# Two RWKV layers: small products of TensorE regrouped, R projections and the bonus term moved earlier, the two halves of the tail set further apart

## The chip, the cores and the metric

One NeuronCore of one Trainium2 chip runs the whole program. The metric is the device time of one execution in microseconds (us). 256 tokens of width 1024 go through four blocks (RWKV, stick-breaking attention, sparse attention, RWKV), each followed by a feed-forward network, and then through two hybrid attention layers. Everything is float32.

## What is computed

The change touches only the two RWKV-7 blocks (16 heads of 64 channels). Cut to what matters:

```python
r, k, v = projections of three mixes of h and its shifted copy      # 1024 x 1024 each
decay = exp(-exp(-softplus(-(w0 + tanh(xw @ w1) @ w2)) - 0.5))      # LoRA of rank 64
a = sigmoid(a0 + (xa @ a1) @ a2)                                    # LoRA of rank 64
g = sigmoid(xg @ g1) @ g2                                           # gate, rank 160 = 128 + 32
kk = k * k_k, divided per head by the root of its sum of squares
state = state * decay - (state @ kk) (kk * a)^T + v k^T             # per token, per head
y = state @ r                                                        # then a norm per head
y = y * ln_w + ln_b + sum(r * k * r_k) * v                           # the bonus term
out = (y * g) @ w_out
```

## The kernel before

The recurrence is done in two chunks of 128 tokens: within a chunk a triangular 128x128 system per head is inverted. Large products are written as three `fp32r` matmuls of a high and a low half (lines 117 to 119), and `wload` (L110, L111) splits each weight block of 128x1024 on ScalarE (`whi`) and VectorE (`wlo`). Plain float32 matmuls are two passes on TensorE each, so the counts of matmul rows below are passes, twice the matmuls in the code. Instructions are written in Python order; the framework's planner then orders each engine's queue by that order and by what its model says is ready, so neighbours in the trace need not be neighbours in the code. One RWKV layer (`rwkv`) goes through these stages:

- **Gate and LoRAs.** `lora1` (L1008) makes the gate's inner product in one go: for each of 8 row blocks k, a matmul with 128 columns of weights and one with 32. Its two sigmoids give `sg1` (128 rows) and `sg2` (32 rows). Then a loop over pairs of channel blocks makes decay and `a` (L1066, L1067) with sigmoids on ScalarE and a scan on VectorE (L1074).
- **K projections.** `kproj(c)` for channel block c is 24 matmuls, a copy and a square on ScalarE, and a matmul with `headsel` (L1126: 8 columns) that adds the squares per head into one PSUM tile of 8 rows for four blocks. `rnorm(j)` turns it into inverse norms, `prep` spreads them with a selection matrix (L1139, L1140).
- **The block loop** (L1195 to L1205) over c = 0 to 7: `prep(c+1)` on VectorE and ScalarE, `amat(c)` (L1165, transposes, masked copies), then a K projection for c = 0 and 1 or an R projection for c = 3 and 6 (`RPC`), then `wmat(c)` (L1184).
- **Inversion.** `inv_diag` inverts 32x32 blocks by a chain of 62 VectorE operations (L1330, L1332), each waiting for the one before. Meanwhile the other six R projections (`rproj`, L1253) and the products `rmat` (L1225) and `rout` (L1237, L1243) run.
- **Merge.** `inv_merge` joins the blocks with small matmuls (L1360, L1374, L1376, L1384, L1387). Between its steps it calls `turn()`, which here makes a quarter of the gate's second product (`gtc`, L1266 with 128 rows and L1267 with 32 rows).
- **Tail.** `rwkv_tail(q)` is a Python generator for each half q of the heads. Half B starts two steps (`RLAG`) after half A. In it the bonus term `bv` is built (L1476, L1478). `ohalf` is the output projection; its first half is handed out two pieces per step (`RFO`) once A is done.

```python
for c in range(RPN, KT):                 # L1251: the six later R projections
    rproj(re, c)
    for _ in range(RFR[c]):
        rph.pop(0)()                     # rmat / rout
```

Of the kernel before, what the change touches and what calls it, by code (L numbers as in the profile page):

```python
# [23 lines left out]
RPC = (3, 6)  # L24
RPN = len(RPC)
RFR = (0, 0, 2, 2, 2, 2, 3, 3)
RLAG, RFA, RFB, RFO = 2, 0, 0, 2
# [4 lines left out]
GTP = {}  # L32
# [10 lines left out]
class Prog:  # L43
# [864 lines left out]
    def rwkv(self, x, i):  # L908
# [13 lines left out]
        with ExitStack() as outer:  # L922
# [13 lines left out]
            sg2 = sp.tile([32, S], F32, name="sg2")  # L936
            rnh = [sp.tile([8, S], F32R, name=f"rnh{j}") for j in range(2)]
            rnl = [sp.tile([8, S], F32R, name=f"rnl{j}") for j in range(2)]
# [7 lines left out]
            with tc.tile_pool(name="ra", bufs=1) as ra:  # L946
# [55 lines left out]
                def lora1(m, w, o, n, stride):  # L1002
                    ps = self.psum("mm")
                    for k in range(KT):
                        t = mix(m, k, "xg_", 8)
                        for q in range(0, n, 128):
                            p = min(128, n - q)
                            mm(ps[:p, q // 128 * S:q // 128 * S + S], w[:, o + k * stride + q:o + k * stride + q + p], t,  # L1008
                               start=(k == 0 and q == 0), stop=(k == KT - 1), skip_group_check=True)
                    return ps  # L1010
# [48 lines left out]
                ps = lora1(5, G1, 0, 160, 160)  # L1059
                act(sg1, ps[:, :S], AF.Sigmoid)  # L1060
                act(sg2, ps[:32, S:], AF.Sigmoid)
                for c0 in range(0, KT, 2):
                    pw, pa = self.psum("mm"), self.psum("at")
                    for c in (c0, c0 + 1):
                        o = (c - c0) * S
                        mm(pw[:, o:o + S], L2[:64, c * 128:(c + 1) * 128], la[:64], start=True, stop=True)  # L1066
                        mm(pa[:, o:o + S], L2[64:, c * 128:(c + 1) * 128], la[64:], start=True, stop=True)  # L1067
                    for c in (c0, c0 + 1):
                        o = (c - c0) * S
                        sg = ra.tile([128, S], F32, name="sg", bufs=2)  # L1070
                        act(sg, pw[:, o:o + S], AF.Sigmoid, bias=C("w0", c))
                        act(aT[:, c], pa[:, o:o + S], AF.Sigmoid, bias=C("a0", c))
                        nc.gpsimd.memset(csT[:, c, 0:1], 0.0)
                        nc.vector.tensor_tensor_scan(csT[:, c, 1:], self.ones, sg, 0.0, op0=ALU.mult, op1=ALU.add)  # L1074
                ctr = csT[:, :, 64:256:128]
# [27 lines left out]
            with tc.tile_pool(name="rb", bufs=2) as rb:  # L1103
                self.table("natural_log_exp_and_others")
                selr = rb.tile([8, 4, 128], F32, name="selr", tag="akk1", bufs=1)
                nc.sync.dma_start(selr, self.a["rw_sel8"])
                sel8 = rb.tile([8, 4, 128], F32R, name="sel8", bufs=1)
# [4 lines left out]
                kw, ssp = [None], [None]  # L1112
                nc.gpsimd.tensor_scalar(ka1, C("k_a", 0, 8), -1.0, 1.0, op0=ALU.mult, op1=ALU.add)

                def kproj(c):
                    if c % 2 == 0:
                        kw[0] = self.wload(self.a["rw_k"][l, c // 2], 2048)
                    if c % 4 == 0:
                        ssp[0] = self.psum("o")[:8, :S]
# [4 lines left out]
                    sq = self.tmp.tile([128, S], F32, name="sq", bufs=2)  # L1124
                    act(sq, ps, AF.Square, scale=C("k_k", c))
                    mm(ssp[0], headsel[:, c % 4], sq, start=(c % 4 == 0), stop=(c % 4 == 3))  # L1126

                def rnorm(j):
                    u = self.tmp.tile([128, S], F32, name="sacc", bufs=2)[:8]
                    ts(u, ssp[0], 1e-24, 2.0 ** 20, op0=ALU.max, op1=ALU.mult)  # L1130
                    rn = self.rstd(u, scale=1.0, eps=0.0, p=8)
# [56 lines left out]
                rp = iter(range(RPN))  # L1188
# [6 lines left out]
                for c in range(KT):  # L1195
# [7 lines left out]
                    elif c in RPC:  # L1203
# [3 lines left out]
                act(scol, scol, AF.Exp)  # L1207
            with ExitStack() as rde:
# [4 lines left out]
                re = rde.enter_context(tc.tile_pool(name="re", bufs=2))  # L1213
# [41 lines left out]
                self.xctx.close()  # L1255
                rt = rde.enter_context(tc.tile_pool(name="rt", bufs=1, side="right"))
                GT = rt.tile([128, KT, S], F32, name="GT")
                g2 = self.wraw.tile([128, WCH], F32, name="wraw")
                nc.sync.dma_start(g2[:, :1024], self.a["rw_g2a"][l])
                nc.sync.dma_start(g2[:32, 1024:], self.a["rw_g2b"][l])  # L1260

                def gtc(c0):
                    pg = self.psum("mm")
                    for c in (c0, c0 + 1):
                        o = (c - c0) * S
                        mm(pg[:, o:o + S], g2[:, c * 128:128 + c * 128], sg1, start=True, stop=False)  # L1266
                        mm(pg[:, o:o + S], g2[:32, 1024 + c * 128:1152 + c * 128], sg2, start=False, stop=True)  # L1267
                    cp(GT[:, c0:c0 + 2], pg.rearrange("p (a b) -> p a b", a=2))
                TT.append(rt.tile([128, 16, 128], F32, name="TT1"))
                act(TT[1], self.ones[:, None, :128].to_broadcast([128, 16, 128]), AF.Copy, scale=0.0)  # L1270
# [5 lines left out]
                self.inv_merge([u.rearrange("p a h t -> p (a h) t") for u in AKB], XNT, TT, sc, lambda: gts.pop(0)())  # L1276

                def chain(q):
                    return self.rwkv_tail(q, rc, rt, l, mu, Vc, AKB[q], KB, TT[q], csT, Rh, N0, W00, WK1, scol, coef, GT,
                                          sc[q], C, og, lambda: [rph.pop(0)() for _ in range(max(0, len(rph) - 8 * (1 - q)))],  # L1280
                                          lambda: [gts.pop(0)() for _ in range(max(0, len(gts) - 2 * (1 - q)))])
                add = lambda c, ps: self.new_x(c, x[c], ps)
                fills = [rph, gts, []]

                def fill(n):
                    for _ in range(n):
                        for f in fills:
                            if f:
                                f.pop(0)()
                                break  # L1290
                A, B, i = chain(0), chain(1), 0
                while A or B:
                    if A:
                        if next(A, 1):
                            A = None
                            fills[2] = self.ohalf(self.a["rw_out"][l], 0, og, add)
                        fill(RFA)
                    if B and i >= RLAG:
                        if next(B, 1):
                            B = None  # L1300
                        fill(RFB if A else RFO)
                    for _ in range(GTP.get(i, 0)):
                        if gts:
                            gts.pop(0)()
                    i += 1
                for f in fills[2] + self.ohalf(self.a["rw_out"][l], 1, og, add):
# [99 lines left out]

    def rwkv_tail(self, q, rc, rt, l, mu, Vc, AKB, KB, TT, csT, Rh, N0, W00, WK1, scol, coef, GT, scr, C, og, need, need_gate):

# [21 lines left out]
        need()  # L1430
# [18 lines left out]
        for g in range(2):  # L1449
# [3 lines left out]
            (nc.vector.tensor_copy if g else cp)(UP[:, 4 * g:4 * g + 4], ps)  # L1453
# [19 lines left out]
        bv = TT.rearrange("p h t -> p (h t)")[:, :1024].rearrange("p (c a e v) -> p c a e v", c=4, a=2, e=2)  # L1473
        for ch in range(2):
            bc = lambda u: u[:, ch, hq].rearrange("p (c e) -> p c e", e=2)[:, :, :, None].to_broadcast([128, 4, 2, 64])
            tt(out=bv[:, :, ch], in0=Vc[:, ch, 512 * q:512 * q + 512].rearrange("p (c e v) -> p c e v", e=2, v=64),  # L1476
                                    in1=bc(mu), op=ALU.add)
            tt(out=bv[:, :, ch], in0=bv[:, :, ch], in1=bc(coef), op=ALU.mult)  # L1478
# [12 lines left out]
        need_gate()  # L1491
# [91 lines left out]
def layout(inp, need=None):  # L1583
# [81 lines left out]
    out["rw_g2a"], out["rw_g2b"] = np.ascontiguousarray(f("rw_g2")[:, :128]), np.ascontiguousarray(f("rw_g2")[:, 128:])  # L1665
# [5 lines left out]
    hsel = np.zeros((128, 4, 8), np.float32)  # L1671
    for ch in range(128):
        for cc_ in range(4):
            hsel[ch, cc_, 2 * cc_ + ch // 64] = 1.0
    out["rw_headsel"] = hsel
    out["rw_sel8"] = np.ascontiguousarray(1024.0 * hsel.transpose(2, 1, 0))
# [42 lines left out]
```

## Time and profile before

| | us |
|---|---|
| median of 3 runs | 1864.0 (1863.23 to 1868.2) |
| the profiled execution, its own time | 1852.14 |
| span of its trace, first to last instruction | 1850.4 |
| first RWKV layer, up to the first matmul of the network after it | 273 |
| second RWKV layer, the same stages | 273 |
| mean granted clock of TensorE, share of 2.4 GHz | 0.952 |

The profiled execution is 0.6% below the median of the runs. The engines are TensorE (PE, its weight loads PEld), VectorE (DVE), ScalarE (ACT), GpSimd (POOL) and SyncE (SP), which issues most of the DMAs. A stage of the trace is read by its windows first (which engine is full), then by the timeline or the chain of waits inside it. In the timeline a row is the start in us, the length in us, the engine, the line, what is written and read, the form, the count, and in brackets the idle time before it and what ended that. Successive matmuls overlap, so the price of one in a stream is the distance between starts.

### The profile page before, as it was taken

To read this page: it belongs to the slowest core of one execution; us is meant where nothing else is said; L and a number is where in the kernel's file an instruction comes from. 1 tells how busy PE (TensorE), PEld (TensorE's weight loads), DVE (VectorE), ACT (ScalarE), POOL (GpSimd) and SP (SyncE) were. 2 spreads that over 40 slices of the span, in tenths; PEclk is the share of its full clock that TensorE was granted. 3 is DMA by queue.
4 is the path that set the end of the run, shared out by engine and by line. 5 is a ranking of instruction groups with operands and counts; after the bars stand their busy time and mean duration, and the time that the engine had idled before them with its cause. 6 is when DMAs were issued, how large, how long until landed. Compare 5 with 4: busy or idle time off the path is not lost.

```text
span 1850.4 us, 34035 instructions
## 1 busy us (share of the span) xinstructions
PE 1756.0 (95%) x13699; PEld 1575.6 (85%) x13699; DVE 1375.6 (74%) x2710; ACT 1013.8 (55%) x1832; POOL 40.5 (2%) x78
## 2 busy tenths in 40 slices
PE   7998989999999999999999989999899998997998
PEld 5677789999899999877999966787899997885876
DVE  8869489866688876799887568686787656676665
ACT  4755345545576455567645445754265445664664
POOL 0003000000000000000000000021000000000000
PEclk9989789999999999999999999886899999998999
DMA  5211138746427855632685542211065455432540
GB/s 214 103 52 55 59 113 323 259 157 228 168 93 279 288 183 172 237 137 92 239 295 191 182 164 102 73 57 47 35 223 188 170 192 193 160 137 91 181 159 23
DMA packets 52841, 292.19 MB, mean 158 GB/s; under 512 B 6611, under 2 KB 9435, under 8 KB 27980
## 3 DMA queue, kind: packets, MB, share of 16 engines
q1 hardware_dynamic: 48540, 284.64, 43.4%
q10 hardware_dynamic: 4144, 5.39, 0.9%
q8 instruction: 107, 1.75, 0.4%
q14 instruction: 50, 0.41, 0.1%
HBM read 287.90 MB, written 2.10 MB: 157 GB/s over the span
## 4 chain that ended last, share of the span: by engine, by line
PE 73%; DVE 14%; DMA 5%; ACT 3%; issue 2%; DVEq 0%; ACTq 0%
PE mm L117 14%; PE mm L118 14%; PE mm L119 14%; PE mm L222 5%; PE mm L223 5%; PE mm L224 5%; DMA adaw<-ada 4%; DVE wlo L111 3%; DVE junk L678 2%; PE o L511 1%; PE at L475 1%; PE mm L1184 1%; PE at L1165 1%; PE mm L1266 1%; PE mm L1267 1%
## 5 line engine op out<-in xcount | busy, mean ns | idle before, releaser
L111 DVE TENSOR_TENSOR wlo<-wraw,whi 128x1024 fp32r<-128x1024 f32 (+2 forms) x518 | 588.3, 1140 | 229.5 <-ACT whi L110 227.3
L110 ACT CAST whi<-wraw 128x1024 fp32r<-128x1024 f32 (+2 forms) x518 | 504.2, 982 | 296.9 <-PE mm L119 174.3
L222 PE MATMUL mm<-whi,xgh 128*128 128x512 f32 x192 | 80.9, 421 | 8.5 <-ACT xgh L737 8.5
L1549 ACT ACTIVATE sg<-gt 128x256 f32<-128x256 f32 x88 | 36.7, 417 | 90.0 <-DVE gt L1546 89.8
L117 PE MATMUL mm<-mh,whi 128*128 128x256 f32 x256 | 80.9, 316 | 5.0 <-DVE Rh L1097 3.8
L118 PE MATMUL mm<-mh,wlo 128*128 128x256 f32 x256 | 77.9, 304 | 0.0
L119 PE MATMUL mm<-ml,whi 128*128 128x256 f32 x256 | 77.8, 304 | 0.0
L223 PE MATMUL mm<-wlo,xgh 128*128 128x512 f32 x192 | 77.2, 402 | 0.0
L224 PE MATMUL mm<-whi,xgl 128*128 128x512 f32 x192 | 77.0, 402 | 0.0
L678 DVE SCALAR_TENSOR_TENSOR junk<-adaw,cs 128x1024 f32<-128x1024 f32 x48 | 58.6, 1221 | 17.9 <-DMA adaw<-ada 17.7
L1546 DVE TENSOR_TENSOR gt<-mm,rr 128x512 f32<-128x512 f32 x88 | 60.5, 687 | 8.5 <-PE mm L119 5.7
L117 PEld LDWEIGHTS mm<-mh,whi 128*128 128x128 f32 x256 | 55.2, 216 | 9.0 <-DVE Rh L1097 4.0
L118 PE MATMUL mm<-xg0h,wlo 128*128 128x256 f32 x192 | 53.8, 280 | 5.2 <-DVE wlo L111 5.1
L118 PEld LDWEIGHTS mm<-mh,wlo 128*128 128x128 f32 x256 | 55.2, 216 | 1.7 <-issue 1.7
L119 PEld LDWEIGHTS mm<-ml,whi 128*128 128x128 f32 x256 | 54.7, 214 | 1.7 <-issue 1.7
L117 PE MATMUL mm<-xg0h,whi 128*128 128x256 f32 x192 | 54.6, 284 | 0.0
L119 PE MATMUL mm<-xg7l,whi 128*128 128x256 f32 x192 | 53.2, 277 | 0.6 <-DVE xg7l L135 0.6
L222 PEld LDWEIGHTS mm<-whi,xgh 128*128 128x128 f32 x192 | 37.4, 195 | 18.9 <-ACT xgh L737 9.4
L117 PE MATMUL mm<-xg4h,whi 128*128 128x256 f32 x192 | 53.5, 278 | 0.0
L117 PE MATMUL mm<-xg7h,whi 128*128 128x256 f32 x192 | 53.2, 277 | 0.0
L119 PE MATMUL mm<-xg0l,whi 128*128 128x256 f32 x192 | 53.1, 277 | 0.0
L117 PE MATMUL mm<-xg1h,whi 128*128 128x256 f32 x192 | 53.1, 277 | 0.0
(831 smaller groups left out, 6067.1 us busy)
## 6 DMA issues: line engine op xcount, KB each, us to landing
wraw<-ffn_gu SPq DMA_DIRECT2D x88, 1024.0 KB, 6.1
wraw<-ffn_dn SPq DMA_DIRECT2D x64, 704.0 KB, 4.0
adaw<-ada SPq DMA_DIRECT2D x48, 512.0 KB, 5.7
wraw<-hy_qkv SPq DMA_DIRECT2D x24, 1024.0 KB, 4.9
wraw<-rw_k SPq DMA_DIRECT2D x8, 1024.0 KB, 4.9
wraw<-rw_r SPq DMA_DIRECT2D x8, 1024.0 KB, 4.9
wraw<-rw_out SPq DMA_DIRECT2D x8, 1024.0 KB, 4.8
wraw<-sb_qk SPq DMA_DIRECT2D x8, 1024.0 KB, 4.8
```

Source lines behind the costliest of these rows:

```text
L110: nc.scalar.copy(hi, rw)
L111: nc.vector.tensor_tensor(out=lo, in0=rw, in1=hi.bitcast(F32), op=ALU.subtract)
L117: mm(ps, w[0], x[0], start=first, stop=False, **kw)
L118: mm(ps, w[1], x[0], start=False, stop=False, **kw)
L119: mm(ps, w[0], x[1], start=False, stop=last, **kw)
L222: mm(ps, x[0], w[0], start=first, stop=False)
L223: mm(ps, x[0], w[1], start=False, stop=False)
L224: mm(ps, x[1], w[0], start=False, stop=last)
L475: nc.tensor.matmul(z[e][:, o:o + n], qT[b, hp, t * 128:t * 128 + 128], kT[b, hp, :n], start=True, stop=True)
L678: nc.vector.scalar_tensor_tensor(out=junk, in0=raw, scalar=1.0, in1=self.cs, op0=ALU.mult, op1=ALU.mult, accum_out=self.mod[l][:, j:j + 1])
L1546: nc.vector.tensor_tensor(out=gt, in0=ps.rearrange("p (a b) -> p a b", a=2), in1=r[:, None, :].to_broadcast([128, 2, S]), op=ALU.mult)
L1549: nc.scalar.activation(sg, gt[:, 0], AF.Silu)
```

## The change

The gate's inner product is cut in four pieces that are spread over the LoRA loop, and its 32-column part is made four times, into PSUM rows 0, 32, 64 and 96. The squares of k stay in the second half of `KB`, and four matmuls with a 32-column `headsel` in `rnorm` write to the four row quarters. `gtc` makes four channel blocks at a time, with the 32-row parts on four row groups and four PSUM tiles. All eight R projections are in the block loop. `GT`, `TT1` and the loads of `g2` come before the `rmat`/`rout` products. The bonus term is made by eight VectorE operations ahead of `inv_turn`, in a pool opened after that of `rmat`/`rout` is closed. `RLAG` goes from 2 to 5.

```diff
-RPC = (3, 6)
+RPC = (0, 0, 1, 1, 1, 1, 2, 2)
-RLAG, RFA, RFB, RFO = 2, 0, 0, 2
+RLAG, RFO = 5, 2
...
-                def lora1(m, w, o, n, stride):
+                def lora1(ps, ks, m, w, o, n, stride):
+                    for k in ks:
+                        xt_ = [(k + j, mix(m, k + j, "xg_", 8)) for j in range(2)]
                         for q in range(0, n, 128):
                             p = min(128, n - q)
+                            for k1, t in xt_:
+                                for g in range(0, 128, p):
+                                    mm(ps[g:g + p, q // 128 * S:q // 128 * S + S], w[:, o + k1 * stride + q:o + k1 * stride + q + p], t,
+                                       start=(k1 == 0 and q == 0), stop=(k1 == KT - 1), skip_group_check=True)
...
-                ps = lora1(5, G1, 0, 160, 160)
+                pg = self.psum("mm")
                 for c0 in range(0, KT, 2):
...
+                    lora1(pg, (c0,), 5, G1, 0, 160, 160)
+                act(sg1, pg[:, :S], AF.Sigmoid)
+                act(sg2, pg[:, S:], AF.Sigmoid)
...
-                    act(sq, ps, AF.Square, scale=C("k_k", c))
-                    mm(ssp[0], headsel[:, c % 4], sq, start=(c % 4 == 0), stop=(c % 4 == 3))
+                    act(KB[:, c, S:], ps, AF.Square, scale=C("k_k", c))
                 def rnorm(j):
+                    ssp = self.psum("o")[:, :S]
+                    for c in range(4):
+                        mm(ssp[32 * c:32 * c + 32], headsel, KB[:, 4 * j + c, S:], start=True, stop=True)
...
-                    elif c in RPC:
+                    for _ in range(RPC[c]):
                         rproj(rb, next(rp))
...
+                def gtc(a):
+                    pg = [self.psum("at")[:, :S] for _ in range(4)]
+                    for j in range(4):
+                        c = 4 * a + j
+                        mm(pg[j], g2[:, c * 128:128 + c * 128], sg1, start=True, stop=False)
+                    for j in range(4):
+                        b = slice(32 * j, 32 * j + 32)
+                        mm(pg[j], g2[b, 1024 + a * 128:1152 + a * 128], sg2[b], start=False, stop=True)
+                    for j in range(4):
+                        cp(GT[:, 4 * a + j], pg[j])
...
-                for c in range(RPN, KT):
-                    rproj(re, c)
-                    for _ in range(RFR[c]):
-                        rph.pop(0)()
+                for j, f in enumerate(rph):
+                    f()
+                    if j == 8:
+                        gtc(0)
+                rex.close()
+                bv = rde.enter_context(tc.tile_pool(name="rv", bufs=1)).tile([128, 2, 4, 2, 2, 64], F32, name="bv")
+                for q in range(2):
+                    for ch in range(2):
...
+                        tt(out=bv[:, q, :, ch], in0=Vc[...], in1=bc(mu), op=ALU.add)
+                        tt(out=bv[:, q, :, ch], in0=bv[:, q, :, ch], in1=bc(coef), op=ALU.mult)
...
-                og, gts = [None] * KT, [lambda c=c: gtc(c) for c in range(0, KT, 2)]
+                og, gts = [None] * KT, [lambda: gtc(1)]
```

The host's layout follows: `rw_g2b` is 128 rows of 256 values instead of 32 of 1024, `rw_headsel` is 128x32, and `rw_sel8` has 128 rows instead of 8.

## Rows read from the trace of the kernel before

**Rows 1.** The page, part 1: busy time, share and instructions of each engine.
```profile
PE 1756.0 (95%) x13699; PEld 1575.6 (85%) x13699; DVE 1375.6 (74%) x2710; ACT 1013.8 (55%) x1832; POOL 40.5 (2%) x78
```
**Rows 2.** Windows: length, busy PE PEld DVE ACT POOL, PEclk, DMA; last row second layer.
```profile
61.50:88.50 27.00, 23.32 (x160) 19.18 (x160) 18.16 (x35) 21.87 (x47) 1.11 (x3) 0.94 0.32 121
88.50:138.40 49.90, 46.52 (x338) 40.19 (x339) 35.49 (x89) 26.81 (x79) 1.03 (x2) 0.83 0.13 46
138.40:181.50 43.10, 37.30 (x344) 35.09 (x343) 41.35 (x84) 25.87 (x60) 17.20 (x19) 0.95 0.18 62
181.50:216.70 35.20, 33.15 (x480) 23.65 (x480) 12.31 (x17) 14.57 (x21) 0.00 (x0) 0.57 0.14 43
216.70:273.20 56.50, 50.88 (x482) 49.13 (x481) 45.93 (x103) 22.52 (x47) 0.00 (x0) 0.91 0.25 96
1174.40:1224.90 50.50, 47.48 (x337) 40.86 (x338) 35.52 (x89) 26.82 (x79) 1.03 (x2) 0.80 0.14 45
```
**Rows 3.** Groups by line, VectorE, inversion (138.4 to 181.55): busy us, mean ns.
```profile
L111 DVE TENSOR_TENSOR wlo<-wraw,whi 128x1024 fp32r<-128x1024 f32 x5 | 6.1, 1216 | 0.0
...
L1097 DVE TENSOR_TENSOR Rh<-mm,E1r 128x256 f32<-128x256 f32 x6 | 2.5, 411 | 0.0
```
**Rows 4.** The chain that ended last, merge: start, us, what.
```profile
183.55 3.82 PE mm L1360 x128
187.37 1.15 PE mm L1266 x2
...
212.27 0.63 PE mm L1266 x2
...
214.77 2.00 PE at L1387 x32
```
**Rows 5.** Windows: most of the merge.
```profile
183.00:211.00 28.00, 27.45 (x414) 19.41 (x416) 8.82 (x14) 12.89 (x19) 0.00 (x0) 0.50 0.12 39
```
**Rows 6.** Timeline of TensorE, tail.
```profile
243.74 1.12 PE L1498 MATMUL mm<-ident,WK 128*128 128x128 f32 x4 [3.38 <-DVE WK L1446]
```
**Rows 7.** Timeline of TensorE: an unbroken float32 stream, and the gate's inner product.
```profile
33.01 3.62 PE L1054 MATMUL mm<-dx,L1m 128*128 128x256 f32 x16
...
47.66 9.39 PE L1008 MATMUL mm<-xm,G 128*128 128x256 f32 x32
```
**Rows 8.** Timeline of TensorE, tail: products that alternate between two column halves.
```profile
228.79 1.09 PE L1468 MATMUL at<-KB,AKB 128*64 128x128 f32 x16
```
**Rows 9.** Timeline of TensorE: head sums among K projections, and the first L1165.
```profile
68.28 0.97 PE L1126 MATMUL o<-sq,rw_headsel 128*8 128x256 f32 x2 [1.96 <-ACT sq L1125]
...
72.63 0.60 PE L1126 MATMUL o<-sq,rw_headsel 128*8 128x256 f32 x2
...
83.26 0.60 PE L1126 MATMUL o<-sq,rw_headsel 128*8 128x256 f32 x2
...
88.52 1.80 PE L1165 MATMUL at<-aT,KB 64*128 64x128 f32 x16 [1.42 <-DVE KB L1155]
```
**Rows 10.** Timeline of TensorE, block loop: five of the wmat groups, one rout.
```profile
94.33 1.00 PE L1184 MATMUL mm<-Vc,akk 128*128 128x64 f32 x8
...
100.84 1.00 PE L1184 MATMUL mm<-Vc,akk 128*128 128x64 f32 x8
...
106.39 0.88 PE L1184 MATMUL mm<-Vc,akk 128*128 128x64 f32 x6
...
114.34 1.00 PE L1184 MATMUL mm<-Vc,akk 128*128 128x64 f32 x8
...
117.17 0.51 PE L1237 MATMUL o<-rkb,prod 128*128 128x2 f32 x4
...
119.38 0.88 PE L1184 MATMUL mm<-Vc,akk 128*128 128x64 f32 x6
```
**Rows 11.** Groups by line, VectorE, tail (216.7 to 258): the bonus term.
```profile
L1476 DVE TENSOR_TENSOR TT<-Vc,mu 128x512 f32<-128x512 f32 x4 | 2.7, 688 | 2.0 <-PE mm L1425 2.0
L1478 DVE TENSOR_TENSOR TT<-TT,coef 128x512 f32<-128x512 f32 x4 | 2.7, 684 | 0.0
```

More of the change, by code (lines that the diff above doesn't have):

```diff
@@ L935, in rwkv @@
             sg1 = sp.tile([128, S], F32, name="sg1")
[L936 to L938 removed]
+            sg2 = sp.tile([128, S], F32, name="sg2")
+            rnh = [sp.tile([128, S], F32R, name=f"rnh{j}") for j in range(2)]
+            rnl = [sp.tile([128, S], F32R, name=f"rnl{j}") for j in range(2)]
             mu = sp.tile([128, 2, 16], F32, name="mu")
@@ L1212, in rwkv @@
                 X = self.inv_diag(rd, AKB)
-                re = rde.enter_context(tc.tile_pool(name="re", bufs=2))
+                rt = rde.enter_context(tc.tile_pool(name="rt", bufs=1, side="right"))
+                GT = rt.tile([128, KT, S], F32, name="GT")
+                TT.append(rt.tile([128, 16, 128], F32, name="TT1"))
+                act(TT[1], self.ones[:, None, :128].to_broadcast([128, 16, 128]), AF.Copy, scale=0.0)
+                g2 = self.wraw.tile([128, WCH], F32, name="wraw")
+                nc.sync.dma_start(g2[:, :1024], self.a["rw_g2a"][l])
+                nc.sync.dma_start(g2[:, 1024:1280], self.a["rw_g2b"][l])
+                def gtc(a):
[8 more added lines that the diff above has]
+                        cp(GT[:, 4 * a + j], pg[j])
+                rex = ExitStack()
+                re = rex.enter_context(tc.tile_pool(name="re", bufs=2))
                 bo = self.psum("o")
@@ L1260, in rwkv @@
[L1260 to L1268, printed above, removed]
@@ L1269, in rwkv @@
-                TT.append(rt.tile([128, 16, 128], F32, name="TT1"))
-                act(TT[1], self.ones[:, None, :128].to_broadcast([128, 16, 128]), AF.Copy, scale=0.0)
+                for j, f in enumerate(rph):
[6 more added lines that the diff above has]
+                    for ch in range(2):
+                        bc = lambda u: u[:, ch, 8 * q:8 * q + 8].rearrange("p (c e) -> p c e", e=2)[:, :, :, None].to_broadcast([128, 4, 2, 64])
+                        tt(out=bv[:, q, :, ch], in0=Vc[:, ch, 512 * q:512 * q + 512].rearrange("p (c e v) -> p c e v", e=2, v=64),
+                           in1=bc(mu), op=ALU.add)
+                        tt(out=bv[:, q, :, ch], in0=bv[:, q, :, ch], in1=bc(coef), op=ALU.mult)
@@ L1282, in rwkv @@
                 add = lambda c, ps: self.new_x(c, x[c], ps)
[L1283 to L1291, printed above, removed]
-                while A or B:
[L1293 to L1304, printed above, removed]
+                A, B, i, rest = chain(0), chain(1), 0, []
@@ L1305, in rwkv @@
+                while A or B:
+                    if A and next(A, 1):
+                        A = None
+                        rest = self.ohalf(self.a["rw_out"][l], 0, og, add)
+                    if B and i >= RLAG and next(B, 1):
+                        B = None
+                    for f in rest[:RFO]:
+                        f()
+                    rest = rest[RFO:]
                     i += 1
-                for f in fills[2] + self.ohalf(self.a["rw_out"][l], 1, og, add):
+                for f in rest + self.ohalf(self.a["rw_out"][l], 1, og, add):
@@ L1429, in rwkv_tail @@
         yield
-        need()
         def y_group(ch, rhs):
@@ L1472, in rwkv_tail @@
         yield
[L1473 to L1478, printed above, removed]
         norm(0)
```

57 lines of the change are left out of this document (19 added, 38 removed).

## The prediction

> **What bounds the kernel now.** I read the page's engine shares first: TensorE is busy 95% of the span, VectorE 74% [rows 1]. The mean hides what matters, because the change touches only two stretches of 273 us each. So I cut the first RWKV layer into stages with the windows view [rows 2]; the second repeats it (its block loop takes 50.5 us against 49.9). K projections (27.0 us) and block loop wait on each other in turns: no engine is full, and the loop's granted clock is 0.83. In the inversion VectorE is full (41.35 of 43.10 us), and 8.6 us of that, 6.1 and 2.5, are not the inversion but weight splits and products for R projections that run beside it [rows 3]. In the merge TensorE counts as busy 33.15 of 35.20 us. The chain of waits shows with what: twelve steps of 1.15 us like the one at 187.37 and four of 0.63 like that at 212.27, together 16.3 us, are quarters of the gate's second product that stand between the small merge steps [rows 4], and at 0.50 granted, the 1.2 GHz level [rows 5]. The tail lasts 56.5 us, of which TensorE is busy 50.88 at 0.91 [rows 2]; its largest hole, 3.38 us, waits for a norm on VectorE [rows 6], where both halves' norms come together.
>
> So three engines' queues take turns, and work is worth moving only out of a stage where its engine ends last into one where it does not. Each term below is for one layer.
>
> **Gate's inner product: 0 us (-2 to +9).** Now 32 passes take 9.39 us, 0.293 each, though an unbroken stream of passes with 256 moving columns runs at 3.62/16 = 0.226 [rows 7]; the difference, 2.2 us in all, goes with the alternation of 128 and 32 columns. The change halves the alternations, but makes 64 narrow passes of the 16. Nothing in the trace runs on four column quarters. The nearest row alternates two column halves: 16 passes of 128 moving columns in 1.09 us, 0.068 each [rows 8], where half of 0.226 is 0.113. Two halves thus run 1.7 times as fast as one after the other. With four quarters I take 3 times: 64 x 0.226 / 3 = 4.8, plus 16 x 0.226 = 3.6, plus half of 2.2, together 9.5 against 9.39. Four times gives 8.3; one after the other gives 64 x 0.226 + 3.6 = 18.1, the upper end. The spreading over the LoRA loop I count as nothing, as its sigmoids and scans go on beside it. It adds one wait: `pg` holds one of three `mm` tiles to the end, so the loop's next `pw` waits for ScalarE one step sooner, with the first K projection queued behind it; a gate piece of 9.5/4 = 2.4 us stands between two such waits and covers them. Without that cover the loop would run at ScalarE's pace, within the +9.
>
> **Head sums: -5.5 us (-3.6 to -7).** Each head sum costs two passes of 0.60 us in the stream [rows 9]; three projections with theirs take (83.26 - 72.63)/3 = 3.54 us, so 2.9 without. The first also waits 1.96 us for ScalarE's square and runs at 0.97. Four sums lie before the norms on which `prep(0)` and the first L1165 (88.52) hang, two more in the stage, two in the loop. Before the norms 4 x 0.60 + 1.96 + 0.37 = 4.7 us go and one set of eight passes is added, 0.6 to 1.8 us; behind them two more sums go, which the chain of norms covers in part. The wait for the square can't come back as such: a square is now read only by `rnorm`, so what is late next is the square of the fourth projection, right before its sums. I take -5.5; passes alone give 6 x 0.60 = -3.6. The larger load of the selection matrix (128 rows instead of 8) is needed only at the first `prep`, some 20 us later, and that stage's DMA share is 0.32: nothing.
>
> **Block loop: +8 us (+2 to +17).** Six R projections come in. Ends of the wmat groups give the length of a block [rows 10]: with a K projection 100.84 - 94.33 = 6.51, with an R projection 114.34 - 106.39 = 7.95, with neither 119.38 - 114.34 = 5.04. TensorE's own work in a block is 117.17 - 114.34 = 2.83 us. If it were packed full, 8 x 2.83 + 10 x 2.9 = 51.6 us, +2 on 49.9: the lower end. If each moved projection costs 7.95 - 5.04 = 2.9, +17: the upper end. I take the K blocks' length, since a block with a projection has TensorE busy and the block that took 7.95 also waited for the second norms: 6 x 6.51 and two blocks with two projections, 6.51 + 2.9 = 9.4 each, make 57.9. VectorE's 35.49 us and the 8.6 that come from the inversion fit in that, as do ScalarE's 26.81 and as many splits and exponentials. The R weights are asked for on SP's queue in the loop, where the DMA share is 0.13; the loads of `g2` behind them come earlier too, ahead of the output weights.
>
> **Inversion: -3 us (-8 to +2).** VectorE loses 8.6 us. It gets the bonus term, eight operations of 0.69 = 5.5 us [rows 11], which lay in the tail, and which stand ahead of the transposes that the merge needs. Their tile takes the place of the tiles of `rmat` and `rout`, so they can't start before the last of these; TensorE's share there falls by six projections (6 x 2.9 = 17 of 37.3 us), so that these should end before the 62-step chain. If the bonus fell wholly into waits, -8; if `rout` ended after the chain and the bonus stood alone, about +2. The quarter-size copies of the gate and the zeroing of `TT1` on ScalarE (25.87 of 43.10 us busy) cost nothing while VectorE ends last. `gtc(0)` takes all four `at` tiles, so the next `rmat` waits for its copies, and `rout` behind that: this too is TensorE's time, and if TensorE ended last, part of the +2.
>
> **Merge: -8 us (-11 to -4).** The 16.3 us of gate steps become one piece at the first `turn`: eight wide passes of 0.575 us (half of 1.15) and eight narrow ones which, four row groups at a time, count as two, 5.75 us. That leaves -10.5. What the pieces hid then shows: the copies between merge steps on ScalarE and VectorE, and the last steps, which now run at the full level behind the pieces (2.00 us at 214.77 [rows 4]), may stay at the half level: I give back 2.5. If all hidden copies show, -4.
>
> **Tail: -4 us (-8 to +4).** The ideal is TensorE without a hole at full level: 56.5 - 50.88 = 5.6 us of holes and some 2.5 us from the granted 0.91, so at best -8. With the halves five steps apart A's norms no longer share VectorE with B's, the bonus (5.5 us) is gone from it, and the first half of the output projection falls between B's last steps. Against it, A's first steps run alone and may start at the half level. I take half. At worst A's lone steps cost what the lag was to save, +4.
>
> **Sum.** 0 - 5.5 + 8 - 3 - 8 - 4 = -12.5 us a layer, -25 for both. The profiled execution takes 1852.1, so 1827; the median of the runs shown is 11.9 higher, 1864.0, and from that I forecast **1839 us**.
>
> **Rivals.**
>
> *A, the clock gives the gain back.* With six projections gone TensorE has about 20 us of work in the 43 of the inversion. Now its granted clock is 0.95 there, and it falls to 0.50 in the merge once TensorE stands still before it [rows 2, 5]. If it drops already in the inversion, `rmat` and `rout` take 2 x 20 = 40 us and end last: -3 becomes 0, and the tail starts low: -4 becomes 0. Per layer -5.5, in all 1853. For it: the merge's 28 us at 0.50. Against it: TensorE need not be fast where VectorE's chain lasts 40 us. The Trainium skill, TensorE: Matmul & The Clock Gate (Why this matters for your kernels), says to leave no idle gaps between bursts in mid-kernel, since the array falls back to half rate; by that rule this rival would be the likeliest. The rows show the low clock behind an idle stretch, so they agree with the rule, but not that this stretch will be one.
>
> *B, column quarters take turns.* Then the gate's product costs +9: -3.5 a layer, 1857. Rows 8 speak against it. The same page (Part 3, What overlaps and what doesn't) says that weight loads overlap running matmuls only where the row group differs, which it does not here, so by it B would hold; this trace's two column halves overlap nonetheless (0.068 against 0.113).
>
> *C, slower: the moved projections lengthen the loop by all they cost at the half level.* The loop's granted clock is 0.83 [rows 2], and a projection at the half level takes 2 x 2.9 = 5.8 us. Six in series give +35 instead of +8, so +14.5 a layer and 1893. It decides from 3.4 us per moved projection, where the loop eats the other 20.5 us. For it: the measured 2.9 was in a partly slowed block. Against it: 6.51 with the K projection, where the engine is kept fed.
>
> *D, the change does little.* The planner orders the queues itself, and may have R projections, gate pieces and bonus end up beside the same work as now: 1864.
>
> **Chances.** Forecast 0.66, A 0.13, B 0.05, C 0.09, D 0.07. A difference under 0.3% (5.6 us) can't be told from none. The forecast is faster but for 0.03 within the bound; A 0.11 faster, 0.02 within; B half and half; D 0.06 within, 0.01 slower; C slower. Rounded: faster 0.77, same 0.13, slower 0.10. The ends of the terms add up to -34 and +24 a layer, which won't all fall together. Half of the way from -12.5 to the low end, in both layers alike, is -23 a layer, 1817; upwards the range goes to 1858 and so takes in A and B. It leaves out C, D and a low tail of 0.04.
>
> **What would show it.** Right: in the changed profile the K stage some 5 us shorter with two groups of head sums per layer; ten projections in the loop and a loop of 55 to 60 us at a granted clock over 0.83; no splits among L1330 and L1332; a single stretch of gate steps in the merge; no hole over 3 us in the tail. Wrong: narrow gate passes at 0.2 us distance (B), a loop over 70 us (C), the last `rout` behind the chain of VectorE (A), or R projections still beside the chain (D).

## The result and the profile after

The changed kernel takes 1832.9 us, median of four runs (1828.3 to 1840.4), against 1863.6 for the kernel before on the same chip: ratio 0.984, 95% interval 0.981 to 0.987. The profiled execution took 1828.3, its span is 1826.5 against 1850.4 us. The forecast was 1839 and faster, the range 1817 to 1858; the sum held, but three of its terms did not.

Windows of the changed kernel: block loop, inversion, merge and tail of the first layer, then of the second. The columns are those of [rows 2].

```profile
85.20:136.90 51.70, 51.68 (x474) 48.26 (x474) 42.59 (x100) 33.15 (x91) 1.03 (x2) 1.00 0.32 112
136.90:185.70 48.80, 34.88 (x257) 30.36 (x256) 38.70 (x84) 23.69 (x59) 14.93 (x19) 0.75 0.13 44
185.70:209.60 23.90, 21.98 (x448) 21.82 (x448) 11.03 (x15) 11.94 (x16) 0.00 (x0) 0.50 0.06 16
209.60:262.30 52.70, 49.82 (x466) 47.33 (x465) 39.05 (x93) 21.40 (x45) 0.00 (x0) 0.94 0.23 84
1158.80:1210.40 51.60, 51.59 (x474) 48.18 (x476) 41.44 (x99) 34.13 (x93) 1.04 (x2) 1.00 0.28 95
1210.40:1257.50 47.10, 35.60 (x256) 31.09 (x256) 40.11 (x83) 22.65 (x58) 14.83 (x19) 0.74 0.13 46
1257.50:1281.50 24.00, 22.03 (x449) 21.84 (x449) 11.06 (x15) 11.94 (x16) 0.00 (x0) 0.50 0.06 17
1281.50:1333.00 51.50, 49.58 (x465) 47.31 (x465) 38.98 (x91) 22.31 (x46) 0.00 (x0) 0.94 0.23 82
```

Set against [rows 2], the loop is 1.8 us longer, with TensorE full and at 1.00 where it was 0.83; the merge 11.2 and the tail 3.9 us shorter; and the inversion, which was to lose 3, has gained 5.6 us. VectorE, full there before, is now idle for 10 of 48.8 us and TensorE's mean clock has fallen from 0.95 to 0.75. What lies ahead of the loop shrank by 3.3 us (the first amat product starts at 85.22, before at 88.52 [rows 9]).

Timeline of TensorE, changed kernel: one of the four gate pieces, the last head sums of the first group, the first amat product, and three wmat groups of blocks with one R projection each.

```profile
48.75 2.13 PE L1006 MATMUL mm<-xm,G 128*128 128x256 f32 x20
...
76.30 0.62 PE L1126 MATMUL o<-KB,rw_headsel 128*32 128x256 f32 x2 [1.40 <-ACT KB L1120]
...
85.22 1.16 PE L1163 MATMUL at<-aT,KB 64*128 64x128 f32 x16 [1.18 <-DVE KB L1153]
...
108.67 1.00 PE L1182 MATMUL mm<-Vc,akk 128*128 128x64 f32 x8
114.19 1.00 PE L1182 MATMUL mm<-Vc,akk 128*128 128x64 f32 x8
119.72 1.00 PE L1182 MATMUL mm<-Vc,akk 128*128 128x64 f32 x8
```

A gate piece lasts 2.06 us to the next start (50.81): 4 wide passes at 0.226 leave 1.16 us for 16 narrow ones, 0.072 each, so column quarters run 3.1 times as fast as one after the other. An R block lasts 5.5 us, where 7.95 was read and 6.5 assumed. The last head sum waits 1.40 us for the square of the fourth projection: the wait named as next in line is there.

The inversion in slices of 5 us, changed kernel, first layer from the end of the loop on:

```profile
136.90:141.90 5.00, 3.01 (x41) 2.80 (x40) 3.29 (x5) 4.39 (x6) 3.30 (x3) 1.00 0.00 0
141.90:146.90 5.00, 2.01 (x12) 1.90 (x12) 2.90 (x6) 4.95 (x11) 1.21 (x2) 0.69 0.00 0
146.90:151.90 5.00, 5.00 (x26) 4.46 (x25) 3.95 (x10) 2.98 (x9) 1.89 (x4) 0.50 0.01 2
151.90:156.90 5.00, 5.00 (x31) 4.54 (x31) 4.62 (x12) 1.75 (x6) 2.14 (x4) 0.50 0.65 213
156.90:161.90 5.00, 5.00 (x27) 4.56 (x28) 4.69 (x10) 1.95 (x6) 1.82 (x3) 0.50 0.00 0
161.90:166.90 5.00, 4.56 (x32) 3.06 (x30) 1.69 (x4) 1.40 (x5) 0.00 (x0) 0.77 0.00 0
166.90:171.90 5.00, 5.00 (x57) 4.62 (x57) 4.38 (x8) 2.94 (x10) 3.00 (x4) 1.00 0.01 3
```

TensorE works 5 of the first 10 us behind the loop, is granted 0.50 (1.2 GHz) for the next 15, and `rmat` and `rout` run at that level; instructions per slice double, from about 28 to 57, when the clock is back. Timeline in this stretch, TensorE, VectorE and ScalarE:

```profile
137.49 1.05 ACT L107 CAST whi<-wraw 128x1024 fp32r<-128x1024 f32 x1 [6.27 <-DMA wraw<-rw_out]
138.44 1.91 ACT L1215 ACTIVATE TT<-ones 128x2048 f32<-128x2048 f32 x1
140.68 4.26 ACT L1315 COPY D__1614<-AKB 32x512 f32<-32x512 f32 x4
...
145.94 1.22 PE L1244 MATMUL at<-Rh,KB 64*128 64x128 f32 x4 [2.26 <-ACT KB L1250]
...
160.57 3.73 PE L1225 MATMUL at<-sg,wraw 128*128 128x256 f32 x8
164.22 0.71 PE L1228 MATMUL at<-sg,wraw 32*128 32x256 f32 x8
...
167.38 0.42 DVE L1247 TENSOR_TENSOR prod<-Rh,KB 128x256 f32<-128x256 f32 x1 [3.69 <-PE o L1256]
...
176.65 0.68 DVE L1279 TENSOR_TENSOR bv<-Vc,mu 128x512 f32<-128x512 f32 x1
```

Three things hold up VectorE's chain: ScalarE's cast and zeroing come ahead of the copies that the chain starts with (it starts 9.6 us behind the loop, before 6.5); `gtc(0)` takes 4.4 us of TensorE at 160.57 while L1247 waits for a product behind it, 3.69 us; and the bonus term's eight operations stand in the chain from 176.65 on. The second `gtc` ran at 173.7 to 177.2, still in the inversion: the merge holds no gate step at all.

### The profile page after: what moved, and what is told of

It is laid out like the page before. It is cut to its first block, busy times and chain, and to the rows that moved or that the text cites. A ratio compares the mean times of both kernels' runs of the same rounds, so it can differ in the third digit from the quotient of the medians.

```text
span 1826.5 us, 34255 instructions
## 1 busy us (share of the span) xinstructions
PE 1731.1 (95%) x13795; PEld 1575.2 (86%) x13795; DVE 1368.8 (75%) x2706; ACT 1019.9 (56%) x1847; POOL 36.0 (2%) x78
## 4 chain that ended last, share of the span: by engine, by line
PE 75%; DVE 14%; DMA 5%; ACT 4%; issue 2%; DVEq 0%; SPq 0%; ACTq 0%
PE mm L114 14%; PE mm L116 14%; PE mm L115 14%; PE mm L219 6%; PE mm L220 5%; PE mm L221 5%; DMA adaw<-ada 4%; DVE wlo L108 4%; DVE junk L675 1%; PE o L508 1%; PE at L472 1%; ACT whi L107 1%; PE at L1163 1%; PE at L1244 1%; PE at L495 1%
## 5 line engine op out<-in xcount | busy, mean ns | idle before, releaser
L114 PE MATMUL mm<-mh,whi 128*128 128x256 f32 x256 | 74.3, 290 | 1.1 <-ACT sg L1072 0.6
L115 PE MATMUL mm<-mh,wlo 128*128 128x256 f32 x256 | 72.0, 281 | 0.0
L116 PE MATMUL mm<-ml,whi 128*128 128x256 f32 x256 | 72.0, 281 | 0.0
L115 PE MATMUL mm<-xg1h,wlo 128*128 128x256 f32 x192 | 53.0, 276 | 0.0
L115 PE MATMUL mm<-xg4h,wlo 128*128 128x256 f32 x192 | 53.0, 276 | 0.0
L116 PE MATMUL mm<-xg4l,whi 128*128 128x256 f32 x192 | 53.0, 276 | 0.0
L114 PE MATMUL mm<-xg5h,whi 128*128 128x256 f32 x192 | 53.0, 276 | 0.0
```

Source lines behind the costliest of these rows:

```text
L114: mm(ps, w[0], x[0], start=first, stop=False, **kw)
L115: mm(ps, w[1], x[0], start=False, stop=False, **kw)
L116: mm(ps, w[0], x[1], start=False, stop=last, **kw)
```

## The experiments

Theory T, from this reading: merge, tail and head sums gave the gain, the six R projections are nearly free in the loop, and the inversion lost 5 us to the three obstacles. Outside the two RWKV layers the same instructions took up to 16 us more in one execution than in another (912.9 against 896.5 us between the layers, distance of the halves 2 against the changed kernel), so I read stages, in both layers, and take spans as a second look. The 896.5 us of the changed kernel are the shortest of all the traces here, so its span flatters it. Each row of stages comes from one trace; the last column has the median time of the program and the number of runs, from several chips on which the medians of the kernel before were 1863.4 to 1868.6. Lengths in us, first / second layer:

| kernel | loop | inversion | merge | tail | program (runs) |
|---|---|---|---|---|---|
| before | 49.9 / 50.5 | 43.2 / 42.3 | 35.2 / 35.1 | 56.6 / 55.8 | 1863.6 (4) |
| changed | 51.7 / 51.5 | 48.7 / 47.2 | 24.0 / 24.0 | 52.7 / 51.5 | 1832.9 (4) |
| gtc(0) first | 51.6 / 51.6 | 54.4 / 43.0 | 22.5 / 22.2 | 50.0 / 49.1 | 1826.1 (2) |
| bonus in tail | 51.7 / 53.2 | 45.0 / 43.7 | 22.3 / 22.3 | 52.8 / 52.2 | 1837.0 (2) |
| halves 2 apart | 51.7 / 51.6 | 48.2 / 47.3 | 24.0 / 24.0 | 56.4 / 57.1 | 1850.3 (6) |
| R beside | 43.5 / 42.2 | 42.3 / 42.3 | 27.9 / 27.9 | 50.2 / 48.8 | 1816.2 (4) |
| R beside, run again | 43.3 / 45.4 | 42.8 / 42.3 | 27.8 / 27.8 | 50.0 / 49.2 | 1814.4 (6) |
| R beside, bonus in tail | 43.8 / 42.3 | 43.2 / 42.5 | 27.7 / 27.8 | 53.2 / 52.1 | 1824.4 (4) |
| R beside, old head sums | 50.0 / 50.2 | 43.2 / 43.2 | 28.1 / 28.9 | 50.0 / 54.4 | 1836.2 (1) |
| bonus in tail, gtc(0) last | 51.7 / 51.7 | 46.1 / 45.0 | 24.1 / 22.9 | 52.9 / 51.8 | 1829.1 (1) |
| gate in the merge | 51.7 / 51.7 | 55.2 / 53.9 | 23.8 / 23.8 | 50.1 / 49.2 | 1851.0 (1) |
| filled | 51.7 / 51.7 | 45.5 / 44.5 | 22.7 / 22.9 | 49.1 / 48.8 | 1826.1 (1) |
| ScalarE's order | 51.5 / 53.2 | 50.8 / 50.9 | 24.0 / 24.0 | 52.9 / 51.6 | 1846.5 (8) |

**gtc(0) first.**

```diff
-                for j, f in enumerate(rph):
+                gtc(0)
+                for f in rph:
                     f()
-                    if j == 8:
-                        gtc(0)
```

> gtc(0), the gate's first half of the second product, runs ahead of the rmat and rout steps instead of between them; nothing else differs from the changed kernel. Theory T (the inversion became 5 us longer because gtc(0) keeps TensorE away from the product that VectorE's L1247 waits for, 3.69 us): that wait falls below 0.5 us, the inversion is 3 to 4 us shorter in each layer (48.7 to about 45), the span 6 to 8 us shorter, about 1820. Rival (ScalarE's or VectorE's own order sets the end, the wait only moves to another place): inversion within 1 us of 48.7, span within 2 us of 1826.5.

In the second layer the stall of VectorE went and the inversion came out at 43.0. In the first VectorE still waits three times for L1256, 5.0 us in all, and 4.67 us before the bonus term, and the stage took 54.4. It is one program, and TensorE and VectorE do the same operations in the same order in this stage of both layers. Two of the waits of VectorE's timeline in the first layer, and then slices of both layers, the first and the last of them 15 us behind the loop:

```profile
161.74 0.43 DVE L1247 TENSOR_TENSOR prod<-Rh,KB 128x256 f32<-128x256 f32 x1 [1.80 <-PE o L1256]
...
182.16 0.69 DVE L1278 TENSOR_TENSOR bv<-Vc,mu 128x512 f32<-128x512 f32 x1 [4.67 <-PE mm L1262]
```

```profile
152.20:157.20 5.00, 5.00 (x36) 4.44 (x34) 4.62 (x12) 1.57 (x5) 1.35 (x2) 0.50 0.10 41
172.20:177.20 5.00, 5.00 (x31) 4.66 (x30) 4.69 (x10) 1.57 (x5) 1.65 (x3) 0.50 0.01 3
...
1232.80:1237.80 5.00, 5.00 (x63) 4.50 (x59) 4.72 (x9) 3.13 (x12) 3.70 (x6) 1.00 0.00 0
```

The first layer's TensorE stays at 0.50 for 41 us (144 to 185); the second's is back at 1.00 some 12 us behind the loop, after 7 us. Neither theory had that: the stage goes with the clock in which `rmat` and `rout` run, and 11 us hang on it. Why the clock came back so much later in the first layer is open.

**Bonus term in the tail.** The eight operations of L1279 and L1281 go back to the place that they had in `rwkv_tail`.

> The bonus term is computed in the tail again, as in the kernel before; the halves stay five steps apart. Theory T (in the inversion its eight operations stand in the chain that sets the end, in the tail there is now room for them): inversion 4 to 5 us shorter, tail 0 to 2 us longer, so 2.5 to 5 us less in each layer, span about 1818. Rival (the term's early place is what shortens the tail): tail 4 us or more longer, layer as long or longer, span 1826 or above.

Inversion 3.6 shorter, merge 1.7, tail +0.1 and +0.6: theory T, in this neighbourhood. The program does not show it: its two runs took 1826.2 and 1847.8 us, and the second layer's loop was 1.7 us longer, which the edit does not explain.

**Halves two steps apart.**

```diff
-RLAG, RFO = 5, 2
+RLAG, RFO = 2, 2
```

> The two halves of the tail are two steps apart again, as in the kernel before, all else as in the changed kernel. Theory T (the tail's 4 us come from the distance of the halves): the norms' wait of about 3.4 us on TensorE is back, tail 3 to 4 us longer in each layer, span 1832 to 1836. Rival (the tail is shorter because the bonus term left it): tail within 1 us of 52.7, span within 2 us of 1826.5.

Tail 3.8 and 5.6 us longer, and no other stage moved. The span, 1850.7, lies far above the forecast, as 16.4 us were lost between the layers; the median of six runs is 17.4 us above the changed kernel's, more than the two tails explain, and the rest is open. The waits of TensorE that [rows 6] showed are back, in this kernel's timeline of TensorE, tail of the first layer:

```profile
237.39 1.12 PE L1486 MATMUL mm<-ident,WK 128*128 128x128 f32 x4 [3.39 <-DVE WK L1441]
240.76 0.66 PE L1486 MATMUL mm<-ident,W 128*128 128x128 f32 x2 [2.25 <-DVE W L1441]
```

**R projections beside the inversion again.**

```diff
-RPC = (0, 0, 1, 1, 1, 1, 2, 2)
+RPC = (0, 0, 0, 1, 0, 0, 1, 0)
+RFR = (0, 0, 2, 2, 2, 2, 3, 3)
...
-                for j, f in enumerate(rph):
-                    f()
+                for c in range(2, KT):
+                    rproj(re, c)
+                    for _ in range(RFR[c]):
+                        rph.pop(0)()
...
```

Not shown: the gate's tile, the zeroing of `TT1` and `gtc(0)` move behind these projections.

> Two R projections in the block loop, six beside the inversion with their weight splits on VectorE, as in the kernel before; the gate's tile, TT1 and gtc(0) come after them. Theory T (in the loop the six are nearly free, because TensorE is packed full there and kept at the full level; beside the inversion their splits, 8.6 us, stand on VectorE): loop 1 to 4 us shorter at a granted clock below 0.95, inversion 5 to 10 us longer, each layer 3 to 7 us longer, span 1832 to 1842. Rival C of the prediction (in the loop they cost what they cost in series): loop 10 us or more shorter, span below 1826.

Theory T falls: 1816.2 us (1810.7 to 1819.6; ratio to before 0.975, 0.972 to 0.978), 13 us less in each layer. Rival C had the span (1808.9), not the loop, which is 8 to 9 us shorter. Windows of the first layer:

```profile
85.70:129.10 43.40, 39.85 (x337) 35.15 (x338) 36.15 (x90) 26.46 (x79) 1.03 (x2) 0.92 0.20 72
129.10:171.40 42.30, 37.81 (x344) 35.68 (x343) 40.50 (x85) 25.09 (x58) 15.78 (x17) 0.92 0.18 63
171.40:199.20 27.80, 25.69 (x499) 23.75 (x498) 17.17 (x24) 16.45 (x30) 1.22 (x2) 0.75 0.25 88
199.20:249.40 50.20, 47.09 (x467) 44.59 (x465) 39.05 (x93) 21.40 (x45) 0.00 (x0) 1.00 0.25 91
```

In the loop the six cost 8.2 and 9.4 us, 1.4 to 1.6 each. Beside the inversion they cost less than nothing: TensorE has 37.81 us of work there and is granted 0.92, and VectorE with all its splits ends after 42.3 us, 4.9 and 6.5 us sooner than without them. Part of that is displaced work, since both gate halves and the bonus term follow the projections and now stand in the merge, which pays 3.9 us; but the row with the bonus term in the tail and `gtc(0)` last shows that the inversion is no shorter without the projections where these are out of VectorE's chain.

In T's place I put T2: the moved projections cost time, the early bonus term perhaps too, and the clock beside the inversion decides.

**R beside, bonus in tail.** Both edits above together.

> Six R projections beside the inversion again and the bonus term in the tail again; head sums, gate pieces, gate rows and the distance of the halves as in the changed kernel. New theory T2 (of the change's parts the R projections and the early bonus term cost time: the loop pays 8 to 9 us for the six, and beside the inversion they fit into VectorE's chain and keep TensorE at the full level; the bonus term's operations hold up the merge or the chain): loop 43, inversion 42 to 43, merge 23 to 25 instead of 27.9 with the bonus term there, tail 50 to 51; each layer 2 to 5 us shorter than with the R projections alone put back, span 1800 to 1806. Rival (the tail has no room for the term once TensorE starts it at the full level): tail 4 us longer than 50, span 1808 to 1812.

The rival was right on the stages: tail 3.1 and 3.3 us longer, merge unchanged. Its span was not: 1827.6 against 1808 to 1812, with 10.6 us more between the layers than in the run with the projections alone put back. With the R projections beside the inversion the early bonus term is worth 3 to 4 us a layer (167.9 against 163.7 and 164.6 against 161.2 from the loop's start to the tail's end); with them in the loop it costs 3 to 5 (177.1 against 171.8, 174.2 against 171.4). So the two parts act on each other: moving the R projections costs 13 us a layer with the bonus term early, and only 3.9 and 6.8 with it in the tail (171.8 against 167.9, 171.4 against 164.6). The merge keeps its 27.7 us without the bonus term, so there it was not in the path.

**R beside, old head sums.**

```diff
+                    sq = self.tmp.tile([128, S], F32, name="sq", bufs=2)
+                    act(sq, ps, AF.Square, scale=C("k_k", c))
+                    mm(ssp[0], headsel[:, c % 4], sq, start=(c % 4 == 0), stop=(c % 4 == 3))
...
-                    for c in range(4):
-                        mm(ssp[32 * c:32 * c + 32], headsel, KB[:, 4 * j + c, S:], start=True, stop=True)
```

> Six R projections beside the inversion again and the head sums as in the kernel before (eight of 0.60 us in the stream, results on 8 rows). Tells where the block loop's 43.4 us come from, against 49.9 in the kernel before with the same projections. T2 (the head sums gave 6 us in the loop, since its first blocks wait for the norms and TensorE falls to the half level there): loop 48 to 50 at a granted clock of about 0.83, K stage 3 to 4 us longer. Rival (the loop's gain comes from the gate pieces or from the order of the R projections): loop 42 to 45.

The loop is at 50.0 and 50.2 again, and the first amat product at 89.51 instead of 85.65. The loop's window is the one of [rows 2], clock and all:

```profile
89.50:139.50 50.00, 46.62 (x338) 40.28 (x339) 35.46 (x89) 26.79 (x79) 1.03 (x2) 0.83 0.13 46
```

So the head sums are worth 6.5 us in the loop, and 4.8 to 8.1 in the second layer, by which run of R beside is taken. Ahead of the loop it is 3.9 us, less sure: with the same code up to there the first amat product came at 85.22 in one execution and at 87.84 in another.

**Bonus in tail, gtc(0) last.** The bonus term is in the tail, and `gtc(0)` follows the whole loop over `rph`.

> R projections in the loop as in the changed kernel, the bonus term in the tail, gtc(0) behind the whole rmat and rout loop: nothing of these stands in VectorE's chain any more. T2 with rival A of the prediction (TensorE is too idle beside the inversion to stay at the full level, and rout at the half level ends late): loop 51.7, inversion 40 to 44 with a granted clock below 0.8, that is no more than 3 us under what it is with the R projections beside it; span 1816 to 1824. Theory T (the emptied inversion pays once nothing is in its way): inversion 34 to 38, span 1806 to 1812.

Rival A, though the stage and the span (1827.4) lie above both forecasts: with the bonus term and `gtc(0)` out of the chain the inversion still takes 46.1 and 45.0 us, at 0.57 in the first layer, more than with the R projections beside it. Not every obstacle is gone: ScalarE's cast and zeroing still come first, and VectorE waits for products at the half level. Timeline of VectorE, first layer:

```profile
164.14 0.79 DVE L1247 TENSOR_TENSOR prod<-Rh,KB 128x256 f32<-128x256 f32 x1 [4.45 <-PE o L1256]
```

**Gate in the merge.**

```diff
-                for j, f in enumerate(rph):
+                for f in rph:
                     f()
-                    if j == 8:
-                        gtc(0)
...
-                og, gts = [None] * KT, [lambda: gtc(1)]
+                og, gts = [None] * KT, [lambda: gtc(1), lambda: gtc(0)]
```

> The changed kernel with both halves of the gate's second product in the merge's turns, gtc(1) first, none among rmat and rout. Theory T for the merge (its 11 us came from the gate steps that left it, because the stage runs at the half level and every step there stands in the path): merge 5 to 8 us longer (24 to 29 to 32), inversion 3 to 4 us shorter. Rival (the merge is short because its own steps wait less, and gate steps fit into its waits): merge at most 2 us longer.

The steps are taken from the end of the list, so `gtc(0)` came first. One half still ran in the inversion (178.12 to 184.2), the other near the end of the merge, and the merge did not grow: 23.8 us, as the clock came back during it and the last steps ran at the full level. The inversion, without a gate piece in its middle, grew by 6.5 us, and VectorE waits 4.46, 1.40 and 5.36 us in it for TensorE. The rival had the merge, for another reason; neither theory had the inversion. A slice of this inversion:

```profile
174.60:179.60 5.00, 5.00 (x22) 4.65 (x21) 1.81 (x4) 1.75 (x6) 1.39 (x2) 0.50 0.02 5
```

35 us behind the loop TensorE still has 0.50, where the changed kernel had 1.00 from 30 us on.

**Filled.** T3 narrows T2 to the clock: TensorE's waits right behind the loop let it fall. To test that by itself, work is added that nobody reads.

```diff
                 for j, f in enumerate(rph):
                     f()
+                    if j in (1, 2):
+                        pd = self.psum("mm")[:, :S]
+                        for _ in range(6):
+                            mm(pd, g2[:, :128], sg1, start=True, stop=True)
```

> The changed kernel with twelve extra products (24 passes of 0.213 us, 5.1 us at the full level, 10.2 at the half level) put between rmat(1) and rout(1), into the stretch of 3 to 9 us behind the block loop in which TensorE waits. Their result is read by nobody; the output is computed as before. Theory T3 (TensorE's waits right behind the loop let the clock fall to 0.50, and rmat and rout at the half level, with gtc(0), hold up VectorE's chain): the slices from 10 to 25 us behind the loop are granted 1.00 instead of 0.50, the last rout ends some 10 us earlier, and the inversion is 2 to 6 us shorter (43 to 47 against 48.7) in spite of the added work. Rival (TensorE has too little to do there anyway, or the chain is not waiting for it): clock 0.50 as before, inversion 48 to 54.

Timeline of TensorE, this kernel, from 2 us behind the loop, and then two slices of the same stretch:

```profile
139.35 2.86 PE L1275 MATMUL mm<-sg,wraw 128*128 128x256 f32 x12
...
146.76 1.97 PE L1262 MATMUL mm<-Vc,ark 128*128 128x64 f32 x8 [4.21 <-POOL ark L916]
148.52 4.95 PE L1275 MATMUL mm<-sg,wraw 128*128 128x256 f32 x12
```

```profile
147.40:152.40 5.00, 5.00 (x16) 4.26 (x16) 4.73 (x13) 1.67 (x3) 1.06 (x2) 0.50 0.04 8
152.40:157.40 5.00, 5.00 (x51) 4.22 (x50) 4.15 (x10) 1.75 (x6) 1.35 (x2) 0.95 0.54 206
```

With 7.8 us more to do, TensorE is back at the full level some 12 us sooner (15.5 us behind the loop against 27.3), and the layers are 8.1 and 6.3 us shorter, inversion, merge and tail each. The span shows only 2.2 of that, as 10.3 us more went by between the layers; the kernel ran once. VectorE's wait at L1247, 3.69 us in the changed kernel, is down to this:

```profile
155.14 0.42 DVE L1247 TENSOR_TENSOR prod<-Rh,KB 128x256 f32<-128x256 f32 x1 [0.61 <-PE o L1256]
```

T3's direction and the inversion's size hold, not its reason in full. The clock fell all the same, behind a wait of 4.21 us that the fill did not reach, and rose earlier. The last `rout` did not end 10 us earlier, but 40.8 us behind the loop against 38.7. The planner also set the small products L1256 apart and VectorE's operations in another order, so not all of the gain need be the clock's.

**ScalarE's order.** The zeroing of `TT1` goes behind the last `rout`, the first cast of the output weights behind the copies L1315.

> The changed kernel with two of ScalarE's steps taken out of the stretch behind the loop: the zeroing of TT1 (1.91 us) goes behind the last rout, the first cast of the output weights (1.1 us) behind the copies for the transpose. T3: VectorE's chain starts 2 to 3 us earlier (9.6 to about 7 us behind the loop) and TensorE's hole there is 2 to 3 us shorter; inversion 2 to 4 us shorter (45 to 47), and 40 to 42 if the clock then stays at the full level. Rival (rout and gtc(0) at the half level end last whenever the chain starts): inversion within 1 us of 48.7.

The chain started 2.3 us earlier, as T3 said, and the stage grew by 2.1 and 3.7 us: four weight splits instead of two (5.3 against 2.5 us) now fell into it, and TensorE stayed at 0.50 until 163 as before. Neither forecast of the stage held, and the median of eight runs is 13.6 us above the changed kernel's.

**The best version again.** The kernel with the R projections beside the inversion, unchanged.

> The kernel with six R projections beside the inversion once more, in more rounds, as the version that beats both: median 1811 to 1820 us, stages as in its first run to 0.5 us. Against it would speak a median within 5 us of the changed kernel's 1832.9.

Median 1814.4 us (1810.5 to 1823.5), ratio to before 0.976 (0.971 to 0.980), 18.5 us under the changed kernel's median, taken on another chip. It beats both. The stages repeat to 0.5 us, as expected, but for the second layer's loop, 45.4 us at 0.85 against 42.2 at 0.96; by that run the six cost 6.1 us there and their move 9.5 us in that layer.

## Why the prediction was right, and where it was not

- **Gate's product, 0.** The factor 3 was right (3.1), rival B wrong. The Trainium skill's rule quoted there, in TensorE: Matmul & The Clock Gate (Part 3, What overlaps and what doesn't), does not hold in this trace: the narrow passes, each with its own weight load over the same 128 rows, came 0.072 us apart, where one after the other takes 0.226. The pieces take 4 x 2.06 = 8.2 us against 9.39, yet with old head sums the first amat product came 1.0 us later than before (89.51 against 88.52); that is less than two executions of the same code differ there.
- **Head sums, -5.5.** Mis-sized: about -3.9 ahead of the loop and -4.8 to -8.1 in it. The failed step is to have counted the two sums in the loop as passes alone. With the old sums the loop's clock is 0.83, with the new ones 0.92 in the first layer; how much of the 6.5 us is the clock's was not tested, as a loop at 0.85 took 45.4 us too.
- **Block loop, +8.** The six projections cost 8.2 and 9.4, as said, but the loop only grew by 1.8, since 6.5 of the head sums' gain lies in it. By the other working, TensorE packed full, 51.6 was named as the lower end: 51.7 is it. Rival C's half level did not come.
- **Inversion, -3.** Wrong in sign: +5.6 and +4.9. The failed step is that work taken from VectorE shortens a stage in which VectorE is full. The chain also waits for small products, and these run at half the clock once the projections have left: the 3.69 us at L1247, and up to 11.2 us where the clock stays low longest. Rival A had the mechanism and put it at 3 us; the stage came out 8 over the forecast, of which the bonus term, taken out again, gives back 3.6. A's own sign did not show: the last `rout` ended at 175.6 and the chain at 185.7, so the products hold the chain up in its middle and not at its end. Here the Trainium skill, TensorE: Matmul & The Clock Gate (Why this matters for your kernels), spoke against the change in its warning of idle gaps in mid-kernel, and the trace bears it out (0.95 to 0.75). Rival A deserved more than 0.13.
- **Merge, -8.** -11.2: no gate piece was left in it, against one in the working. At 0.50 throughout, as assumed. That the leaving steps made the gain is read from the trace; putting them back did not show it, as the clock changed with them.
- **Tail, -4.** -3.9 and -4.3, and the distance of the halves alone is 3.8 and 5.6. No hole over 3 us is left, as said; the largest is 1.05. The stage starts at the half level, with a mean clock of 0.94; the kernels with 1.00 there and the bonus term early take 49 to 50 us.
- **Sum, -12.5 a layer.** -11.0 and -11.5, near the forecast by luck, as errors cancel: head sums 5 better, merge 3 better, inversion 8 worse. What the sum hid is that the R projections' move costs 10 to 13 us a layer as the change has it, 6 to 9 in the loop, 5 to 6.5 in the inversion and 2.5 in the tail, of which the merge gives back 3.9. No rival had it: C priced the same move in the wrong stage.

## What to carry to other kernels

Before work is moved out of a stage, ask what it did for the engine that it leaves: the R projections kept TensorE near the full level (0.92 to 0.98 against 0.57 to 0.85) for the small products on which VectorE's chain waits. An engine that is full in a stage is not all that ends last there; look which of its operations wait for another engine, and what these waits become at half the clock. And after a change of several parts that works, undo each alone, and in pairs where they meet: here one part cost over a third of what the rest gained (18 of 49 us), and its price hung on where another part stood.

## What the runs showed of the hardware that I had not expected

- The same program took 54.4 and 43.0 us for the same stage in two layers, with TensorE at 0.50 for 41 us on end in the one, and for 7 and then 14 in the other.
- 7.8 us of added products went with layers 8.1 and 6.3 us shorter.
- Four column quarters ran 3.1 times as fast as one after the other (0.072 us a pass), two column halves 1.7 times [rows 8].
